# A recurrence's twenty head sums, set into a stream of projections in pairs

## The chip, the cores and the metric

The kernel runs on one core of one Trainium2 chip. The metric is the device time of one execution in microseconds (us), where lower is better. A core has engines with instruction streams of their own: TensorE (PE, with its weight loads as PEld), VectorE (DVE), ScalarE (ACT), GpSimd (POOL) and SyncE (SP, which mostly issues DMAs). [...] An instruction that waits holds up everything behind it on its engine.

## The reference

One layer of a hybrid diffusion backbone is applied to 128 context tokens and to 512 latent tokens. The kernel lays them out as 640 tokens, five tiles of 128. Cut to what matters here:

```python
proj = h @ lw['w_in']
(a_x, a_b, a_c, b_q, b_ff, b_fb, b_i, b_g, c_q, c_k, c_v, d_u, d_v) = jnp.split(proj, IN_SPLITS, axis=-1)
y_a = a_b * dwconv3(a_c * a_x, lw['conv_a_w'], lw['conv_a_b'])
y_b, s_f, s_b = hgrn2_bidir(b_q, b_ff, b_fb, b_i, b_g, lb_f, lb_b, ...)    # the recurrence
...                                                                        # y_c attention, y_d gMLP
merged = g_a * (y_a @ w_br_a) + g_b * (y_b @ w_br_b) + g_c * (y_c @ w_br_c) + g_d * (y_d @ w_br_d)
x = x + g1 * (merged @ lw['w_o'])
x = x + g2 * conv_ffn(rmsnorm(x, ...) * (1.0 + sc2) + sh2, ...)
```

`hgrn2_bidir` is a gated linear recurrence in both directions over four heads of 64. With decays f = exp(log_f), its output is, for each token t, a sum over earlier tokens s of (q_t · k_s · product of the decays between them) times v_s, plus the same from later tokens, plus what the carried state of 64 x 64 gives. The final context states are an output too.

## The kernel before, in words

All matrix products of the layer are made from split f32 operands: a weight tile is split into a high and a low part (`w`, split by ACT at L323 or L336 and by DVE at L324 or L337), activations into `XH` and `XL`, and three matmuls make one product. The input projections `h @ w_in` come first. They run section by section (`in_tile`, through `gemm_half`, whose matmuls are recorded at L375, 320 tokens wide) and for the sections `i` and `dv` token by token (`tok_tile`, L947, 256 wide).

The mixers are written as Python generators that are advanced while the projections are issued: after each group of three projection matmuls, the code calls `tick(us)` with the time that these three are planned to take (0.41 in `gemm_half`, 0.33 in `tok_tile`). `tick` moves a planned clock on and advances each generator whose next step is due. A generator's `yield x` says that its next step is due x planned us (times a slack factor, 1.3 for the recurrence) after its present one. So a generator's yields decide behind which projection matmul its next instructions stand. The instruction order that results is then fixed, apart from what the tile framework's own scheduler exchanges among ready instructions. Small products take a PSUM buffer from a pool of four (`pm`, tile names `m_…`), the projections from a pool of two (`g_…`).

Several generators share this stream. `hgrn` is the recurrence and starts when its `q` section is done. `ada_cols` makes modulation columns: weight tiles are loaded by SP and multiplied and summed on DVE at L285, 1.2 us each. `gmlp` is the chunked gMLP (L694, L704, L709), and `attn` the attention, which is started behind the last input section and is the next large user of PE (L762 onward).

The recurrence works by doubling: level l joins blocks of 2^l tokens into blocks twice as long. Its steps, in the order of the code:

- the products of keys and queries, on DVE (L469 to L491);
- `along(ksum)`, and from its result the diagonal of the block matrix on DVE (L497);
- level 0: `along(near)`, and a masked copy by DVE into the same block matrix (L520);
- levels 1 to 6: products of keys and queries on PE (L539), a masked copy of each on DVE (L544) or a copy on ACT (L548), then the updates of the decayed keys, queries and decays on DVE (L558, L562) and copies of keys (L506 on DVE, L507 on ACT);
- the state, for four pairs of tiles: `kt_load` transposes two key tiles on PE (L578), ACT copies each (L581), `upd` multiplies them with the values on PE (L587), and DVE adds each result to the decayed state (L598; the context's copies at L595);
- the outputs of five token tiles on PE (L632, L634, L639), copied and squared on ACT (L643, L644), normalised with DVE and POOL (L648, L318, L623), then transposed (L661) and gated (L665), and stored (L668).

`along(x)` makes ten head sums: each is one matmul with a 128 x 128 tile of `x` as weights and the two columns of `heads` as moving operand (L479, 128x2). All ten fall into one PSUM buffer, which DVE reads once, after the tenth. It is called twice, so there are twenty sums. At `yield 0.5`, a step is due 0.65 planned us after the one before.

Of the kernel before, what the change touches and what calls it, by code (L numbers as in the profile page):

```python
# [70 lines left out]
def tile_step(ctx: ExitStack, tc: tile.TileContext, a: dict, outs: list, dbg=None):  # L71
# [21 lines left out]
    def pe(us):  # L93
        now[0] += us
# [38 lines left out]
    def pm():  # L133
        return psm.tile([P, 512], F32, tag="m", name=nm("m"))
# [74 lines left out]
    for x in LORD.split():  # L209
        if x[0] == "w":  # L210
            i, h = int(x[1]), int(x[2])
# [248 lines left out]
    def hgrn():  # L460
# [13 lines left out]
        def along(x):  # L474

            m = pm()
            mv = m[:, 0:20].rearrange("p (r i) -> p i r", r=2)
            for i in range(10):
                mm(mv[:, i, :], x[:, i * P:(i + 1) * P], heads, start=True, stop=True)  # L479
                pe(0.22)  # L480
                yield 0.5
            return m


# [5 lines left out]
        for j in range(2):  # L490
            vec.tensor_tensor(n2[:, j], k2(j)[:, j], q2(1 - j)[:, 1 - j], ALU.mult)  # L491
        dm = yield from along(ksum)

        near_at = hd[:, 1280:1920].rearrange("p (r i t) -> p r i t", r=2, i=10)
# [17 lines left out]
        for l in range(7):  # L512
# [5 lines left out]
            if l == 0:  # L518
                m = yield from along(near)
                vec.copy_predicated(nat, lmask[:, 0, :].unsqueeze(1).to_broadcast([P, 20, 32]), bc(m))  # L520
# [1943 lines left out]
```

## Time and profile before

| what | value |
|---|---|
| median of 3 runs | 1006.01 us (1005.86 to 1006.21) |
| the profiled execution's own time | 1005.19 us |
| its span | 1003.4 us |
| granted TensorE clock in each stage from 78 us on | 1.00 |
| PE busy | 992.1 us, 99% of the span, 7509 matmuls |
| DVE busy | 823.6 us, 82% |
| ACT busy | 559.4 us, 56% |
| POOL busy | 165.8 us, 17% |
| the twenty head sums on PE | first call 78.9 to 84.1 us, second call 92.0 to 102.0 us |

The span lies between the first and the last recorded work; 1.8 us of the execution's time lie outside it. A timeline row reads: start, time, engine, line, operation, output<-input, shapes, and how many such instructions stand together. A bracket behind it gives the idle time of the engine ahead of it and what ended that. One f32 head sum shows as two matmuls in the trace.

### The profile page before, as it was taken

What the parts mean: (1) busy time and instruction counts of PE and PEld (TensorE: products, weight loads), DVE (VectorE), ACT (ScalarE), POOL (GpSimd) and SP (SyncE); (2) the same over time, 40 slices, a digit from 0 to 9 for tenths busy, and PEclk for the clock granted to TensorE, in tenths of its full rate; (3) what the DMA queues carried; (4) which work ended last, traced back from release to release, by engine and by line L of the source; (5) the groups of instructions that cost most, each with busy time, mean ns of one, the idle gap of its engine ahead of it and who ended that gap; (6) DMA issues with size and microseconds to landing.
All of it is one profiled execution on the core that took longest, in us unless ns stands there. A gap on an engine that the chain in (4) does not pass through costs nothing.

```text
span 1003.4 us, 18971 instructions
## 1 busy us (share of the span) xinstructions
PE 992.1 (99%) x7509; PEld 941.0 (94%) x7509; DVE 823.6 (82%) x1383; ACT 559.4 (56%) x983; POOL 165.8 (17%) x223
## 2 busy tenths in 40 slices
PE   8999999999999999999999999999999999999997
PEld 6899999999999999999998899999999999888886
DVE  6678899867766767777768878999999998999796
ACT  6642343444544544445545376777777777756672
POOL 1000020323120221341010021222222222100004
PEclk9999999999999999999999999999999999999998
DMA  9875343497485498898259675766666666975842
GB/s 354 333 251 160 116 148 123 127 253 226 106 282 201 159 252 180 271 291 182 93 173 347 277 290 170 229 154 174 174 161 171 177 169 194 364 259 205 298 134 105
DMA packets 69865, 208.93 MB, mean 208 GB/s; under 512 B 9616, under 2 KB 24752, under 8 KB 67088
## 3 DMA queue, kind: packets, MB, share of 16 engines
q1 hardware_dynamic: 43392, 148.60, 41.7%
q0 software_dynamic: 26384, 59.12, 25.3%
q8 instruction: 59, 0.97, 0.4%
q14 instruction: 30, 0.25, 0.1%
HBM read 165.99 MB, written 48.51 MB: 214 GB/s over the span
## 4 chain that ended last, share of the span: by engine, by line
PE 93%; DVE 3%; DMA 2%; issue 1%; POOL 1%; ACT 1%; SPq 0%; POOLq 0%; ACTq 0%; DVEq 0%
PE g L1523 21%; PE m L1152 17%; PE g L375 15%; PE m L1995 9%; PE m L1523 5%; PE g L1165 5%; PE g L1995 4%; PE m L1295 3%; PE g L947 2%; PE g L1295 2%; PE m L151 2%; PE g L151 1%; PE m L539 1%; PE m L1518 1%; DMA A<-in_w_ada_dram 1%
## 5 line engine op out<-in xcount | busy, mean ns | idle before, releaser
L375 PE MATMUL g<-XH,w 128*128 128x320 f32 x704 | 171.2, 317 | 0.1
L375 PEld LDWEIGHTS g<-XH,w 128*128 128x128 f32 x704 | 120.6, 188 | 2.7 <-issue 1.0
L375 PE MATMUL g<-XL,w 128*128 128x320 f32 x352 | 108.7, 309 | 0.0
L375 PEld LDWEIGHTS g<-XL,w 128*128 128x128 f32 x352 | 66.3, 188 | 0.0
L1995 PE MATMUL m<-w,XH 128*128 128x512 f32 x246 | 58.5, 390 | 0.0
L1995 PEld LDWEIGHTS m<-w,XH 128*128 128x128 f32 x246 | 46.1, 188 | 9.6
L1152 PE MATMUL m<-XH,w 128*128 128x320 f32 x224 | 52.5, 309 | 0.0
L151 POOL DMA_DIRECT2D wsum<-in_w_dn_dram x36 | 36.5, 1164 | 53.2 <-issue 42.3
L151 DVE SCALAR_TENSOR_TENSOR X<-MG,p2t,X 128x641 f32<-128x641 f32 x44 | 38.9, 884 | 1.0 <-ACT X L151 0.2
L151 ACT ACTIVATE w<-raw 128x1024 fp32r<-128x1024 f32 (+3 forms) x46 | 38.2, 851 | 2.6 <-DMA raw<-in_w_in_dram 1.5
L151 DVE SCALAR_TENSOR_TENSOR X<-X,p2t,X 128x641 f32<-128x641 f32 x44 | 38.9, 883 | 0.9
L1523 PE MATMUL g<-XL,w 128*128 128x320 f32 x240 | 38.7, 310 | 0.0
L1152 PEld LDWEIGHTS m<-XH,w 128*128 128x128 f32 x224 | 38.3, 188 | 0.0
L1523 PE MATMUL g<-XL,C 128*128 128x320 f32 x240 | 38.3, 309 | 0.0
L1523 PEld LDWEIGHTS g<-XL,w 128*128 128x128 f32 x240 | 36.0, 188 | 0.6 <-ACT MG L151 0.3
L1523 PEld LDWEIGHTS g<-XL,C 128*128 128x128 f32 x240 | 36.0, 188 | 0.0
L151 ACT ACTIVATE ga<-m,cst 128x320 f32<-128x320 f32 x27 | 14.2, 528 | 36.6 <-PE m L1152 36.6
L1152 PE MATMUL m<-XL,w 128*128 128x320 f32 x112 | 34.6, 309 | 0.0
L151 DVE TENSOR_TENSOR w<-raw,w 128x1024 fp32r<-128x1024 f32 (+2 forms) x36 | 30.6, 871 | 1.3 <-ACT w L151 1.2
L151 DVE TENSOR_TENSOR gb<-g,gb 128x640 f32<-128x640 f32 x12 | 9.9, 825 | 26.3 <-PE g L1165 25.4
L1894 DVE TENSOR_TENSOR w<-raw,w 128x1024 fp32r<-128x1024 f32 (+1 forms) x26 | 29.0, 1114 | 2.6 <-ACT w L1890 2.6
L336 ACT ACTIVATE w<-raw 128x1024 fp32r<-128x1024 f32 (+1 forms) x22 | 24.3, 1104 | 12.2 <-PE m L947 8.2
(591 smaller groups left out, 2918.4 us busy)
## 6 DMA issues: line engine op xcount, KB each, us to landing
wsum<-in_w_dn_dram POOLq DMA_DIRECT2D x30, 512.0 KB, 11.8
raw<-in_w_up_dram SPq DMA_DIRECT2D x30, 512.0 KB, 5.1
raw<-in_w_gp_dram SPq DMA_DIRECT2D x21, 640.0 KB, 6.7
raw<-in_w_in_dram SPq DMA_DIRECT2D x19, 512.0 KB, 4.2
H<-in_w_adt_dram SPq DMA_DIRECT2D x19, 512.0 KB, 3.8
raw<-wsum SPq DMA_DIRECT2D x12, 512.0 KB, 5.4
actx<-X POOLq DMA_DIRECT2D x22, 256.0 KB, 4.9
wsum<-wsum POOLq DMA_DIRECT2D x10, 512.0 KB, 11.0
```

The costliest lines, as they stand in the source:

```text
L151: r = f(*args, **kw)
L336: high = lambda: act(w[:, 0], raw, AF.Copy)
L375: mm(o, w[:, h, k0 + k, :], r(k)[:, s], start=(k == 0 and i == 0), stop=(k == kt - 1 and i == 2))
L539: mm(m[W * g:W * g + W, (i - s0) * W:(i - s0 + 1) * W], lhs, rhs, start=True, stop=True, tile_position=(64 * par, W * g))
L947: mm(o, x(kx)[:, ts], w[:, h, k, :], start=(kx == 0 and i == 0), stop=(kx == 7 and i == 2))
L1152: mm(o, w[:, k, :], x[:, k, :], start=(first and k == 0 and j == 0), stop=(k == 3 and j == 2), skip_group_check=True)
L1165: mm(pb[:, c, 0:HC], w[:, h + k, :], y[:, x, k, s], start=(k == 0 and j == 0), stop=(k == 1 and j == 2))
L1295: mm(m, mh[k // 2][:, hx, k % 2, t * P:(t + 1) * P], wo[q][:, hw, k % 2, :], start=(k == 0 and i == 0), stop=(k == 7 and i == 2))
L1518: mm(o, w[:, k, :], x[:, k, :], start=(first and not part and k == 0 and j == 0), stop=(part == 1 and k == 3), skip_group_check=True)
L1523: z = mm(o, w[:, k, :], x[:, k, :], start=(first and k == 0 and j == 0), stop=(k == 3 and j == 2), skip_group_check=True)
L1894: vec.tensor_tensor(w[:, 1, 0:n], raw, w[:, 0, 0:n].bitcast(F32), ALU.subtract)
L1995: mm(ps, s[t // 4][:, hx, k, o:o + P], w[:, hw, k, c0:c1], start=first, stop=i == 2 and bi == len(batch) - 1 and k == len(ks) - 1, skip_gr ...
```

## The change

The pause behind each sum is replaced by one behind each second sum. `[1.2] * (i % 2)` is empty for even i and one element for odd i, so that two sums are issued in one step, and the next step is due 1.2 x 1.3 = 1.56 planned us later.

```diff
             for i in range(10):
                 mm(mv[:, i, :], x[:, i * P:(i + 1) * P], heads, start=True, stop=True)
                 pe(0.22)
-                yield 0.5
+                yield from [1.2] * (i % 2)
             return m
```

In the second call the projections around the sums are those of L375. In PE's order before, each sum (L479) stands alone between projection matmuls:

```order
L375 MATMUL g_1190<-XH_255,w_1012 128x320
L479 MATMUL m_1230<-heads,E_1020 128x2
L375 MATMUL g_1190<-XH_255,w_1012 128x320
L375 MATMUL g_1190<-XL_15_256,w_1012 128x320
L375 MATMUL g_1190<-XH_255,w_1012 128x320 x2
L375 MATMUL g_1190<-XL_16_257,w_1012 128x320
L375 MATMUL g_1190<-XH_255,w_1012 128x320
L479 MATMUL m_1230<-heads,E_1020 128x2
L375 MATMUL g_1190<-XH_255,w_1012 128x320
```

The same place in PE's order of the changed kernel (`m_1230` is the one PSUM buffer of the ten sums, `E_1020` holds `near`):

```order
L479 MATMUL m_1230<-heads,E_1020 128x2 x2
L375 MATMUL g_1190<-XH_255,w_1012 128x320
L375 MATMUL g_1190<-XL_15_256,w_1012 128x320
L375 MATMUL g_1190<-XH_255,w_1012 128x320 x2
L375 MATMUL g_1190<-XL_16_257,w_1012 128x320
L375 MATMUL g_1190<-XH_255,w_1012 128x320 x2
L375 MATMUL g_1190<-XL_16_257,w_1012 128x320
L375 MATMUL g_1190<-XH_255,w_1012 128x320
L479 MATMUL m_1230<-heads,E_1020 128x2 x2
```

Ten single sums with six projection matmuls between them have become five pairs with nine. The last sum of the second call stands 18 projection matmuls earlier than before. In the first call, amid `tok_tile`, the sums stand almost where they stood. What follows the second call moves with it: the products of levels 1 to 5 (L539) stand about 15 projection matmuls earlier. On DVE this moves the masked copies of level 1 (L544) against the rest of its order; this is the difference there, with - for before and + for the changed kernel:

```order
 L558 TENSOR_TENSOR B_797<-B_797,A_796 128x320x2 x2
 L506 COPY E_1020<-B_797 128x160x4
-L544 COPY_PREDICATED D_943<-lmask,m_1400 128x320
-L337 TENSOR_TENSOR w_1494<-raw_1258,w_1494 128x1024
-L544 COPY_PREDICATED D_943<-lmask,m_1445 128x320
+L544 COPY_PREDICATED D_943<-lmask,m_1382 128x320
+L544 COPY_PREDICATED D_943<-lmask,m_1427 128x320
 L558 TENSOR_TENSOR C_1037<-C_1037,A_796 128x320x2 x2
 L562 TENSOR_TENSOR A_796<-A_796 128x640
-L285 SCALAR_TENSOR_TENSOR junk_1531,ar_1532<-H_1265,S_82_887 128x1024
 L558 TENSOR_TENSOR B_797<-B_797,A_796 128x160x4
```

The subtraction that makes a low weight part (L337) now stands behind both masked copies and the updates. The third place is the first pair of the state update on PE. Before, the four transposes (L578) stand together, and twelve projection matmuls separate them from the products (L587):

```order
L578 MATMUL m_2331<-cst,B_797 128x128 x2
L578 MATMUL m_2335<-cst,B_797 128x128 x2
L375 MATMUL g_2347<-XH_255,w_1992 128x320
L375 MATMUL g_2347<-XL_15_256,w_1992 128x320
L375 MATMUL g_2347<-XH_255,w_1992 128x320 x2
L375 MATMUL g_2347<-XL_15_256,w_1992 128x320
L375 MATMUL g_2347<-XH_255,w_1992 128x320 x2
L375 MATMUL g_2347<-XL_15_256,w_1992 128x320
L375 MATMUL g_2347<-XH_255,w_1992 128x320 x2
L375 MATMUL g_2347<-XL_15_256,w_1992 128x320
L375 MATMUL g_2347<-XH_255,w_1992 128x320
L587 MATMUL m_2365<-E_1020,D_943 128x128 x2
```

In the changed kernel:

```order
L578 MATMUL m_2303<-cst,B_797 128x128 x2
L375 MATMUL g_2219<-XH_255,w_1874 128x320 x2
L375 MATMUL g_2219<-XL_15_256,w_1874 128x320
L578 MATMUL m_2307<-cst,B_797 128x128 x2
L587 MATMUL m_2324<-E_1020,D_943 128x128 x2
L375 MATMUL g_2219<-XH_255,w_1874 128x320
L587 MATMUL m_2331<-E_1020,D_943 128x128 x2
L375 MATMUL g_2219<-XH_255,w_1874 128x320
L375 MATMUL g_2219<-XL_16_257,w_1874 128x320
L375 MATMUL g_2219<-XH_255,w_1874 128x320
L578 MATMUL m_2349<-cst,B_797 128x128 x2
```

The two transposes of each tile now stand apart, and the first product directly behind the second tile's transposes. Over all, the steps of the state update and the outputs stand 2 to 4 us' worth of projection matmuls earlier. The attention (L762) stands behind the same projection matmul as before. No instruction of the computation is added or removed.

## The prediction

> **What bounds the kernel now.** I read the page first: the busy shares, and the shares of the chain that ended last.
>
> ```profile
> PE 992.1 (99%) x7509; PEld 941.0 (94%) x7509; DVE 823.6 (82%) x1383; ACT 559.4 (56%) x983; POOL 165.8 (17%) x223
> PE 93%; DVE 3%; DMA 2%; issue 1%; POOL 1%; ACT 1%; SPq 0%; POOLq 0%; ACTq 0%; DVEq 0%
> ```
>
> TensorE has matmuls for 99% of the span and carries 93% of the last chain. The waits of PE over the whole run come next (waiting, releaser, total us, times, longest):
>
> ```profile
> PE g L151 <- DVE F L151: 1.6, 1, 1.6
> PE m L151 <- DMA A<-in_w_ada_dram: 1.5, 2, 0.8
> PE m L151 <- DVE X L151: 1.1, 4, 0.3
> PE m L661 <- DVE MG L665: 0.2, 1, 0.2
> ```
>
> That is 4.4 us in all. Only the last, 0.2 us, lies where the recurrence runs. By stages (length, then busy time of PE, its loads, DVE, ACT and POOL, then granted clock, DMA share, GB/s):
>
> ```profile
> 78.00:104.00 26.00, 26.00 (x201) 26.00 (x200) 21.96 (x36) 6.68 (x11) 0.00 (x0) 1.00 0.49 155
> 104.00:160.00 56.00, 55.90 (x1205) 51.25 (x1205) 52.36 (x96) 24.76 (x51) 5.17 (x6) 1.00 0.40 125
> 160.00:190.00 30.00, 30.00 (x235) 29.87 (x235) 27.50 (x70) 9.08 (x26) 2.02 (x2) 1.00 0.41 126
> 190.00:208.00 18.00, 17.84 (x124) 17.41 (x123) 13.49 (x31) 9.04 (x18) 8.39 (x8) 1.00 0.72 195
> ```
>
> From 78 to 208 us, in which everything lies that the change moves, PE idles 0.10 + 0.16 = 0.26 us, and the granted clock is 1.00 throughout. DVE is nearly full there too: 52.36 of 56 and 27.50 of 30. So the time of this stretch is what its matmuls cost back to back. A new order can change it in three ways only: by what the matmuls cost in that order, by taking away 0.26 us of idling, or by making PE wait. The attention behind it stands behind the same projection matmul as before, so a recurrence that ends earlier does not bring the attention forward.
>
> **The sums themselves.** A projection matmul's price comes from two runs of them in the chain (start, us, what, how many), 21.12/144 = 0.147 us and 5.75/48 = 0.120 us:
>
> ```profile
> 49.63 21.12 PE g L375 x144
> 103.64 5.75 PE g L947 x48
> ```
>
> A sum alone, and a pair that the scheduler had already put together in the first call, from PE's timeline:
>
> ```profile
> 96.44 0.28 PE L479 MATMUL m<-heads,E 128*128 128x2 f32 x2
> 96.58 0.39 PE L375 MATMUL g<-XH,w 128*128 128x320 f32 x1
> 96.81 0.31 PE L375 MATMUL g<-XL,w 128*128 128x320 f32 x1
> ...
> 80.11 0.50 PE L479 MATMUL m<-heads,D 128*128 128x2 f32 x4
> 80.48 0.37 PE L947 MATMUL g<-w,XH 128*128 128x256 f32 x1
> 80.68 0.28 PE L947 MATMUL g<-w,XL 128*128 128x256 f32 x1
> ```
>
> I count from start to start. From the single sum to the second projection matmul behind it are 96.81 - 96.44 = 0.37 us, of which 0.147 is the first one's regular price: the sum costs 0.22. Of that, 0.14 is its own, and 0.08 is the return, since the first projection matmul behind it takes 0.23 and not 0.147. The pair: 80.68 - 80.11 = 0.57, less 0.12, makes 0.45. So two sums together cost as much as two apart. Ten singles were 2.2 us and five pairs are 2.25: **+0.05**. The lower bound is that each pair saves a whole return, 5 x 0.08: -0.4. The upper one is +0.05, since nothing in these rows makes a pair dearer than measured. I take +0.05, because its row shows the very thing that is added.
>
> [...]
>
> **The steps behind the sums.** These stand earlier among the projections, 15 matmuls at levels 1 to 5 (15 x 0.147 = 2.2 us) and up to 24 in the state update (3.5 us). The same matmuls are still issued; what was behind them is now ahead. Two things cost. The scheduler splits groups: between the first sum and the attention, PE returns to the projections, not counting the sums, 38 times before and 43 times now. Five returns at 0.08 are **+0.4**. The bounds are 0, if the displaced steps only trade one return for another, and +0.5 by the dearest return in the rows below (164.38 - 164.14 = 0.24, so 0.09 over the regular price, rounded up to 0.1 each).
>
> The second thing: the first product of the state (L587) stands three projection matmuls behind the transposes it depends on, through ACT's copy (L581), where twelve stood before. From the timelines of PE and ACT:
>
> ```profile
> 163.79 0.60 PE L578 MATMUL m<-cst,B 128*128 128x128 f32 x4
> 164.14 0.40 PE L375 MATMUL g<-XH,w 128*128 128x320 f32 x1
> 164.38 0.30 PE L375 MATMUL g<-XL,w 128*128 128x320 f32 x1
> ...
> 165.99 0.72 PE L587 MATMUL m<-E,D 128*128 128x128 f32 x5
> ...
> 171.71 0.68 PE L578 MATMUL m<-cst,B 128*128 128x128 f32 x4
> ```
>
> ```profile
> 172.18 0.69 ACT L581 ACTIVATE D<-m 128x256 f32<-128x256 f32 x2 [3.29 <-PE m L578]
> ```
>
> ACT begins 172.18 - 171.71 = 0.47 after the transposes began, and two copies take 0.69, so the first is there about 0.47 + 0.38 = 0.85 us after them (0.38 being an estimate, half of 0.69 and a little overlap). PE takes 0.35 for four transposes, so 0.18 for two, then 0.08 + 3 x 0.147, then 0.18 for the second tile: it arrives after about 0.88. The copy and its signal come about there: between 0 and 0.4 of waiting. I take **+0.2**. What goes: the 0.26 us of idling, by at most all of it; I take **-0.2**.
>
> **What hides the rest.** PE can only stay full if DVE follows, since the small PSUM buffers come free through DVE. Three of DVE's waits of over a microsecond between 78 and 190 us, and then some of its timeline:
>
> ```profile
> DVE D L544 <- PE m L539: 2.5, 1, 2.5
> DVE w L337 <- ACT w L336: 1.2, 1, 1.2
> DVE D L520 <- PE m L479: 1.2, 1, 1.2
> ```
>
> ```profile
> 164.57 1.22 DVE L285 SCALAR_TENSOR_TENSOR junk<-X,S 128x1024 bf16<-128x1024 f32 x1
> ...
> 169.52 2.37 DVE L598 SCALAR_TENSOR_TENSOR D<-D,tot,m 64x64 f32<-64x64 f32 x8
> ...
> 178.50 2.07 DVE L598 SCALAR_TENSOR_TENSOR D<-D,tot,m 64x64 f32<-64x64 f32 x7
> ```
>
> The first state product starts at 165.99, and DVE takes it up at 169.52: DVE is 3.5 us behind PE there, and only the four buffers keep PE going. If PE comes up to 3.5 us earlier and DVE does not, PE waits. But DVE was late because it had waited itself, 2.5 us for the first product of level 1 and 1.2 us for a weight's high part. The first shrinks by the 2.2 us that PE comes earlier; the second goes, as that subtraction now stands behind both masked copies. So DVE comes 2.2 + 1.2 = 3.4 us earlier. The first buffer that is reused belongs to the third pair of transposes (171.71 before, 24 matmuls earlier now: 168.2). It comes free with the first half of the first L598, 169.52 + 1.19 = 170.7 before, 167.3 now. That leaves 0.9 us, and **0** is what I enter. ACT (9.08 us of 30) and the queues (DMA share 0.40 to 0.41 up to 190 us) have room. SP and POOL keep their instructions; their orders differ only from about 100 to 270 us, where loads of modulation weights and the store of y_b, now some 4 us earlier, fall into 0.41 and 0.72 of the DMA engines.
>
> The sum: +0.05 + 0.4 + 0.2 - 0.2 + 0 = +0.45 us. On the profiled execution, 1005.19 us, of which the span is 1003.4, that makes 1005.64. That execution lies 0.82 below the median of the runs, 1006.01, so against medians I expect 1006.5 us. A measurement here tells about 0.2%, 2 us, from no change. The forecast's own range is 1005.2 (sums at -0.4, returns and copy at 0, all idling gone, so 1006.01 - 0.66, and 0.15 for the spread of the runs shown) to 1007.0 (+0.05 + 0.5 + 0.4 = +0.95).
>
> **The rivals.**
>
> *PE waits for DVE in the state update (slower).* Place: the third pair of transposes. If DVE gains nothing, because its 52 us of work in the levels fill the time and the products of L285 (1.22 us each) slip ahead of the recurrence's own steps, as three of them would to use up 3.4 us, PE waits from 168.2 to 170.7, 2.5 us. The later waits are not added to this: the output's first matmul on the last state needs 178.50 + 2.07 = 180.57, and PE is then no earlier than that. So 1006.46 + 2.5 = 1009.0 us. It begins once DVE gains under 2.5 us there, and passes 2 us in all once DVE gains under about 1. For it: DVE's busy share, and that the order of its products and of the weights' subtractions is changed over 80 us. Against: the removed waits are DVE's own, and no L285 is added before the first L598.
>
> *The lead is kept to the end (faster).* The 2.2 us by which level 1 comes earlier would shorten the run if something behind the recurrence waited for it: 1006.0 - 2.2 = 1003.8. Against: PE idles 0.16 us from 190 to 208, so nothing waits there to be released.
>
> [...]
>
> *The change does less than it says.* In the first call the scheduler had joined sums already (80.11, four matmuls), and there nothing moves. If the splits on PE cost nothing either, 1006.0.
>
> **How the numbers follow.** My forecast has a chance of 0.60, the free pair 0.05 and the idle change 0.05; all three lie within 0.2%: 0.70. PE waiting for DVE has 0.22, as the reserve is only 0.9 us, less than one L285, and rests on an order of some 200 instructions on DVE that no trace here shows. The kept lead has 0.08, including any gain whose way I don't see. The range goes from 1005.2, the forecast's lower end, to 1009.2, which takes in most of the slower case; it leaves out the faster one and the part of the slower where waits add up, under 0.2 together.
>
> **What would show it.** In the changed profile, PE should have about 130 us busy from 78 to 208 with under 0.5 us idle. L479 pairs should take 0.45 us each, ending about 2.6 us earlier (18 x 0.147). The first L544 should start near 109.1 and the first L598 near 166, with no wait of PE on DVE at L578 or L587 above 0.3 us. A wait of PE at L578, L587 or L632 for L598 of a microsecond or more makes me wrong on the slow side; the attention's first L762 more than 1 us earlier makes me wrong on the fast side.

## The result and the profile after

The changed kernel takes 1011.69 us (median of 4 runs, 1009.33 to 1012.66) against 1005.93 us before (4 runs). The ratio is 1.0059, with a 95% interval of 1.0047 to 1.0071: slower by 5.8 us (0.6%), where I had forecast 1006.5 and a range up to 1009.2. The profiled execution is the one of 1012.66 us; its span is 1010.9 us, 7.5 longer than before. Busy shares on the page first:

```profile
PE 995.7 (98%) x7509; PEld 943.7 (93%) x7509; DVE 825.0 (82%) x1383; ACT 560.0 (55%) x983; POOL 166.8 (17%) x223
```

The same 7509 matmuls, but PE is busy for 3.6 us more, so some of them ran slower; the other half of the 7.5 us must be idling. PE's waits of the changed kernel between 78 and 210 us say where:

```profile
PE m L661 <- DVE MG L665: 2.1, 1, 2.1
PE m L539 <- issue: 1.7, 1, 1.7
```

Before, there was one row of 0.2 us. The stages carry the rest of it; the column to read is the granted clock, the third from the right:

```profile
78.00:104.00 26.00, 26.00 (x201) 26.00 (x200) 22.57 (x37) 6.68 (x11) 0.00 (x0) 1.00 0.47 152
104.00:160.00 56.00, 54.20 (x1175) 49.86 (x1173) 51.17 (x87) 24.67 (x51) 5.09 (x6) 0.97 0.35 115
160.00:190.00 30.00, 30.00 (x236) 28.70 (x236) 28.49 (x74) 9.40 (x25) 1.85 (x1) 1.00 0.38 122
190.00:208.00 18.00, 15.86 (x104) 15.48 (x103) 13.69 (x35) 6.53 (x13) 8.59 (x8) 0.94 0.72 206
```

The stage with the pairs is as full as before, at full clock. The losses lie in the two stages behind it: 1.8 and 2.1 us of idling, and in both a clock below 1. PE's timeline at the first stop, inside a group of 80 small products of level 1, and the clock behind it:

```profile
109.56 0.74 PE L539 MATMUL m<-C,D 64*32 64x32 f32 x62
112.00 0.37 PE L539 MATMUL m<-C,D 64*32 64x32 f32 x18 [1.70 <-issue]
```

```profile
113.00:114.00 1.00, 1.00 (x9) 1.00 (x8) 1.00 (x2) 0.00 (x0) 0.00 (x0) 0.77 0.06 16
114.00:116.00 2.00, 2.00 (x12) 1.94 (x11) 1.97 (x3) 0.36 (x1) 0.00 (x0) 0.50 0.00 0
116.00:117.00 1.00, 1.00 (x6) 1.00 (x6) 0.77 (x2) 0.85 (x2) 0.00 (x0) 0.53 0.00 0
```

The releaser "issue" means that the profile shows nothing that holds PE in these 1.70 us: no semaphore, no buffer. After that the clock column shows 0.50; the trace's clock records put this window from 113.53 to 116.94 us, 3.41 us. The projection matmuls in it start 0.213 us apart (three from 114.29 to 114.93 us), where they start 0.120 us apart at full clock:

```profile
114.29 0.41 PE L947 MATMUL m<-w,XL 128*128 128x256 f32 x1
114.50 0.63 PE L947 MATMUL m<-w,XH 128*128 128x256 f32 x2
114.93 0.41 PE L947 MATMUL m<-w,XL 128*128 128x256 f32 x1
```

So PE does 3.41 x 0.120 / 0.213 = 1.9 us' worth of work in the window, and the window costs 1.5 us. The second stop is at the transposes, again with a window of 3.41 us at half clock behind it (205.7 to 209.1 us):

```profile
204.46 0.33 PE L661 MATMUL m<-cst,MG 128*128 128x128 f32 x1 [2.14 <-DVE MG L665]
```

```profile
205.00:206.00 1.00, 1.00 (x9) 0.99 (x8) 0.98 (x5) 0.20 (x1) 0.00 (x0) 0.84 1.24 367
206.00:208.00 2.00, 2.00 (x10) 1.92 (x9) 0.67 (x3) 2.00 (x5) 1.41 (x2) 0.50 0.95 389
208.00:209.00 1.00, 1.00 (x5) 1.00 (x5) 0.35 (x1) 0.88 (x2) 0.17 (x1) 0.50 0.46 184
```

1.7 + 2.1 of stops and 2 x 1.5 of half clock are 6.8 of the 7.5 us. The other 0.7 is about what e5 below shows the new order to cost where nothing stops. Some landmarks, as PE's timelines give the first matmul of a line (us):

```
                        before   after   after again (e11)   both edits (e5)
L539, level 1           110.40  108.18        108.17             108.16
L661, transposes        200.50  200.65        198.96             202.00
L762, attention         208.69  216.24        213.04             209.48
L1152                   308.97  316.53        313.35             309.77
```

Level 1 comes 2.2 us earlier, as worked out. That the figure fits is partly chance: level 1 stands 18 projection matmuls earlier and not 15, and those just ahead of it are of the 0.120 us kind (18 x 0.120 = 2.2); levels 3 to 5 stand 15 earlier. At the attention everything lost is there, and from L762 to L1152 both take 100.28 or 100.29 us.

Why does DVE come late to the transposes? Its timeline before, and then the changed kernel's:

```profile
196.48 0.42 DVE L623 TENSOR_TENSOR MG<-MG,hss 128x256 f32<-128x256 f32 x1 [0.93 <-POOL hss L318]
196.82 1.49 DVE L676 TENSOR_TENSOR E<-X,E 128x1280 fp32r<-128x1280 f32 x1
198.23 1.22 DVE L285 SCALAR_TENSOR_TENSOR junk<-H,S 128x1024 bf16<-128x1024 f32 x1
...
201.08 1.13 DVE L665 SCALAR_TENSOR_TENSOR MG<-m,cst,MG 128x128 f32<-128x128 f32 x3
```

```profile
198.13 0.43 DVE L623 TENSOR_TENSOR MG<-MG,hss 128x256 f32<-128x256 f32 x1 [0.89 <-POOL hss L318]
...
201.32 1.22 DVE L285 SCALAR_TENSOR_TENSOR H<-H,S 128x1024 f32<-128x1024 f32 x1
...
202.79 1.22 DVE L285 SCALAR_TENSOR_TENSOR junk<-A,S 128x1024 bf16<-128x1024 f32 x1
203.93 0.08 DVE L285 DVE_READ_ACCUMULATOR junk<-A,S 128x1 f32 x1
204.05 2.27 DVE L665 SCALAR_TENSOR_TENSOR MG<-m,cst,MG 128x128 f32<-128x128 f32 x8
```

From the last L598 to the first L665, DVE has eight products of L285 in the changed kernel and six before. Two more (2.4 us) have slipped in there, the last one directly ahead of L665. The first of PE's transposes stands 27 projection matmuls earlier, the one that waits 22 earlier than the one that waited before. It waits for the PSUM buffer that L665 has to read.

### The profile page after: what moved, and what is told of

The parts are those of the page before. It is cut to its first block, busy times and chain, and to the rows that moved or that the text cites. A ratio compares the mean times of both kernels' runs of the same rounds, so it can differ in the third digit from the quotient of the medians.

```text
span 1010.9 us, 18975 instructions
## 1 busy us (share of the span) xinstructions
PE 995.7 (98%) x7509; PEld 943.7 (93%) x7509; DVE 825.0 (82%) x1383; ACT 560.0 (55%) x983; POOL 166.8 (17%) x223
## 4 chain that ended last, share of the span: by engine, by line
PE 95%; DMA 2%; DVE 1%; issue 1%; ACT 1%; POOL 0%; SPq 0%; POOLq 0%; ACTq 0%; DVEq 0%
PE g L1523 21%; PE m L1152 17%; PE g L375 16%; PE m L1995 9%; PE m L1523 5%; PE g L1165 5%; PE g L1995 4%; PE m L1295 3%; PE g L947 2%; PE g L1295 2%; PE m L151 2%; PE g L151 1%; PE m L539 1%; PE m L1518 1%; DMA A<-in_w_ada_dram 1%
## 5 line engine op out<-in xcount | busy, mean ns | idle before, releaser
L375 PE MATMUL g<-XH,w 128*128 128x320 f32 x704 | 170.3, 318 | 0.1
L375 PEld LDWEIGHTS g<-XH,w 128*128 128x128 f32 x704 | 121.2, 189 | 2.7 <-issue 1.0
L375 PE MATMUL g<-XL,w 128*128 128x320 f32 x352 | 109.9, 312 | 0.0
L375 PEld LDWEIGHTS g<-XL,w 128*128 128x128 f32 x352 | 66.8, 190 | 0.2
L1152 PE MATMUL m<-XH,w 128*128 128x320 f32 x224 | 52.5, 309 | 0.0
L1523 PE MATMUL g<-XL,w 128*128 128x320 f32 x240 | 38.6, 310 | 0.0
L1523 PE MATMUL g<-XL,C 128*128 128x320 f32 x240 | 38.3, 309 | 0.0
L1152 PEld LDWEIGHTS m<-XH,w 128*128 128x128 f32 x224 | 38.3, 188 | 0.0
L1523 PEld LDWEIGHTS g<-XL,w 128*128 128x128 f32 x240 | 35.9, 188 | 0.7 <-ACT MG L151 0.3
L1523 PEld LDWEIGHTS g<-XL,C 128*128 128x128 f32 x240 | 36.0, 188 | 0.0
L1152 PE MATMUL m<-XL,w 128*128 128x320 f32 x112 | 34.6, 309 | 0.0
```

The lines of the kernel that those rows point to most:

```text
L375: mm(o, w[:, h, k0 + k, :], r(k)[:, s], start=(k == 0 and i == 0), stop=(k == kt - 1 and i == 2))
L1152: mm(o, w[:, k, :], x[:, k, :], start=(first and k == 0 and j == 0), stop=(k == 3 and j == 2), skip_group_check=True)
L1523: z = mm(o, w[:, k, :], x[:, k, :], start=(first and k == 0 and j == 0), stop=(k == 3 and j == 2), skip_group_check=True)
```

## The experiments

Theory A: the loss is the two stops and the half clock behind them. Theory B: the pairs, or the split groups on PE, cost it. Theory C: the stop at L539 hangs on its place in the work (a load, a buffer), and not on the instruction fetch.

**e1: single sums, as early as the pairs.** First, pairing is taken apart from earliness.

```diff
-                yield from [1.2] * (i % 2)
+                yield 0.5 if x is ksum else (0.25, 0.25, 0.5, 0.25, 0.25, 0.5, 0.25, 0.25, 0.5, 0.95)[i]
```

> Ten single sums, as in the kernel before, but issued at the pace that brings the tenth to where the pairs bring it; everything behind the sums stands where the changed kernel has it. Theory A (the loss comes from two stops of PE behind the sums, one in the products of level 1 and one at the transposes L661, and from the half clock behind each): as slow as the changed kernel, 1009 to 1012.7 us, with a stop of about 2 us at L661 and, in most executions, one of about 1.7 us at L539. Theory B (the pairs themselves cost it): as fast as before, 1006 us.

1012.29 us, ratio 1.0065 (1.0052 to 1.0078). PE's waits from 78 to 215 us:

```profile
PE m L661 <- DVE MG L665: 2.2, 1, 2.2
PE m L539 <- issue: 1.3, 1, 1.3
```

Without a single pair in the second call, the loss is all there, at the same two places. Theory B falls for the pairs.

**e9: pairs, with all else in place.** The converse: pairs in the second call, their last where the last single sum was.

```diff
         def along(x):
-
+            yield from [0.5] * (x is not ksum)
...
-                yield from [1.2] * (i % 2)
+                yield from [0.5] if x is ksum else [1.45 if i < 9 else 0.8] * (i % 2)
```

> The kernel before with the ten sums of the second call as five pairs, spaced so that the tenth sum and all that follows it stand where they stand in the kernel before. Theory A (the pairs cost nothing, what moved behind them did): 1005 to 1005.8 us, no stop of PE between 78 and 208 us. Theory B (the pairs cost it): 1006.5 us or more.

1005.16 us against 1005.21, ratio 0.9999 (0.9990 to 1.0007). The stretch as a whole:

```profile
78.00:208.00 130.00, 129.74 (x1758) 124.53 (x1758) 115.28 (x230) 49.58 (x103) 15.54 (x16) 1.00 0.47 141
```

So pairs as such cost and save nothing.

**e4 and e7: the transposes moved.** In e4 they go back in the changed kernel; in e7 they come forward in the kernel before. Both are one number.

```diff
 # e4, in the changed kernel
-HY = 5
+HY = 8
 # e7, in the kernel before
-HY = 5
+HY = 2
```

> The changed kernel with HY = 8 in place of 5: the transposes L661 stand 30 projection matmuls later, 3 behind their place in the kernel before; the level products stay early. Theory A: the stop at L661 goes with the half clock behind it, some 3.8 us less than the changed kernel in the same execution conditions, and what is left is the stop at L539: 1006.5 to 1010 us. Theory B: no change against the changed kernel, 1009 to 1012.7 us.

> The kernel before, single sums, with HY = 2 in place of 5: only the transposes L661 stand earlier, by 27 projection matmuls (4.0 us), as in the changed kernel, and one L285 slips ahead of the first L665 on DVE. Theory A: a stop at L661 of 3 to 4.5 us, more than in the changed kernel since DVE has not come earlier here, often with half clock behind it: 1008.5 to 1011.5 us. Theory B: 1005 to 1006 us.

e4: 1008.80 us, ratio 1.0033 (1.0023 to 1.0044). The stop at L661 is gone, that at L539 is there (1.6 us); the time is 3.5 us below e1's, which was measured in the same series and has both stops. e7: 1012.39 us, ratio 1.0068 (1.0054 to 1.0082), beyond what I expected (1011.5 at most, with a stop of 3 to 4.5 us), by one stop and its clock:

```profile
PE m L661 <- DVE MG L665: 5.2, 1, 5.2
```

```profile
201.00:204.00 3.00, 0.76 (x3) 0.76 (x4) 2.62 (x8) 0.00 (x0) 0.00 (x0) 0.51 1.01 310
204.00:207.00 3.00, 3.00 (x14) 2.85 (x14) 1.33 (x5) 0.00 (x0) 1.42 (x2) 0.50 0.85 320
```

That shows the cause of the second stop from both sides: transposes 4 us earlier, with a DVE that does not follow. The length of e7's stop is the sum of both. Its first L665 starts at 202.84 us against 201.08 before; everything in that profile stands 0.67 us later from the second call of sums on, so DVE is 1.1 us late, with seven L285 in place of six ahead of L665. The delay of 1.09, the 27 projection matmuls at 0.147 (3.97) and the wait of before (0.16) are 5.2 us.

**e2 and e3: the code moved.** Both leave the order alone and change only how many instructions stand ahead of it, by PE's warm-up matmuls at the start.

```diff
 # e2, in the changed kernel
-WARM = 100
+WARM = 118
 # e3, in the kernel before
-WARM = 100
+WARM = 82
```

> The changed kernel with 118 in place of 100 warm-up matmuls at the very start, which PE spends waiting for data anyway: 36 instructions more ahead of everything, so that the level-1 products stand to PE's 16 KB instruction fetches as they do in the kernel before. Theory A, with the stop at L539 being a late instruction fetch: that stop goes, with the half clock behind it, some 3.5 us; PE then comes to L661 earlier, and the stop there grows by up to what DVE has not gained, so 1007 to 1010 us. Theory C (the stop at L539 comes from something that hangs on the place in the projections, such as a load or a buffer): it stays, 1009 to 1012.7 us.

> The kernel before with 82 in place of 100 warm-up matmuls: 36 instructions fewer, so that its level-1 products stand to the instruction fetches as they do in the changed kernel; the order of all else is that of before. Theory A: a stop of 1 to 2 us at L539 with half clock behind it appears, 1008.5 to 1010 us. Theory C: unchanged, 1006 us.

e2: 1013.52 us, ratio 1.0071 (1.0055 to 1.0088). The stop at L539 is gone, that at L661 is unchanged:

```profile
PE m L661 <- DVE MG L665: 2.2, 1, 2.2
PE m L539 <- DVE C L558: 0.3, 1, 0.3
```

The time missed its expectation all the same: it is no lower than e1's 1012.29 us in the same series, which has both stops. So e2 shows what the stop at L539 hangs on, and not that the kernel gains without it. Its profiled execution (1010.48 us) has a window at half clock at 81.7 us, in the first call of sums, with no stop ahead of it, and loses another 0.9 us behind 840 us, where PE waits twice for 0.2 us at L1523. Its slower runs are not explained by that profile. e3: 1006.07 us, ratio 1.0006 (0.9997 to 1.0014). A stop appears at L539 where before had none, but of 0.3 us and without half clock, so the expected 1008.5 was missed. In theory A's favour is the place, against my size for it the length.

**e6 and e10: pairs that come later, and their code moved.**

```diff
 # e6 and e10
-                yield from [1.2] * (i % 2)
+                yield from [1.45] * (i % 2)
 # e10 also
-... tu1a warm24 xo0b ...
+... tu1a warm34 xo0b ...
-WARM = 100
+WARM = 118
```

> The pairs as in the changed kernel, but with 1.45 in place of 1.2, one group of projection matmuls more between them: the tenth sum of the second call stands 6 projection matmuls behind its place before, the level-1 products 15 behind, the first L661 9 behind. Theory A: no stop at either place, 1005 to 1006.5 us. Theory B: the pairs cost as in the changed kernel, 1009 us or more.

> The pairs with 1.45, which had a stop of 1.8 us in the products of level 2, with 28 more warm-up matmuls at the start (118 in place of 100, 34 in place of 24): 56 instructions more ahead of everything, so that level 2 begins 29 instructions behind the place where the fetch that ran late begins, and not 27 ahead of it. Theory A (late instruction fetch): no stop in level 1 or 2, 1005 to 1007 us. Theory C (a load, a buffer or DVE behind the stop): the stop stays at the same matmul of level 2, 1007 to 1009.6 us.

e6: 1008.51 us, ratio 1.0031 (1.0020 to 1.0043); e10: 1009.20 us, ratio 1.0035 (1.0023 to 1.0047). Both missed their times, and both by a stop with the releaser "issue" at a new place, the first of level 2, the second of level 5:

```profile
121.54 0.84 PE L539 MATMUL m<-C,E 64*32 64x32 f32 x75
124.19 0.32 PE L539 MATMUL m<-C,E 64*32 64x32 f32 x5 [1.80 <-issue]
```

```profile
147.57 0.84 PE L539 MATMUL m<-C,B 64*32 64x32 f32 x74
149.86 0.26 PE L539 MATMUL m<-C,B 64*32 64x32 f32 x6 [1.46 <-issue]
```

The trace also records the transfers of instructions (`q8 instruction: 59, 0.97, 0.4%` in the DMA view of both kernels: packets, MB, share of 16 engines). They are 59 of 16,384 bytes in the kernel before and in the changed one, where PE has some 15,100 recorded instructions: one transfer for 256 on average. The record names no engine for them; from this quotient I take them for PE's, and call them fetches. I counted PE's recorded instructions (matmuls, weight loads and its few semaphore instructions) up to three events:

```
kernel       dense group(s) begin   fetch begins at      PE stops at
before       1987                   1952 (108.07 us)     no stop
e2, e5, e8   1987                   1950 to 1952         no stop at level 1
e9           1987                   1974 (109.21 us)     no stop
after        1951                   2123 (109.58 us)     2240
after again  1951                   2063 (108.65 us)     2240
e1, e4       1951                   2113, 2114           2240
e3           1951                   1951 (110.11 us)     2240 (0.3 us)
e6           2436, level 2          2658 (121.76 us)     2752
e10          3718, level 5          3883 (147.22 us)     4032
```

Every stop with the releaser "issue", in seven profiles, falls on 2240 plus a multiple of 256: 2752 is 2 x 256 further, 4032 is 7 x 256. As 256 is also the number of instructions to one transfer, I take PE to have stood there for want of instructions; that is inferred from the counts, and no record shows it directly. It speaks against theory C that e10 took the stop away from level 2 by 56 instructions at the start, some 100 us earlier. Why it happens here I read from a projection matmul's 0.147 us and a level product's 0.011 us (80 in 0.89 us): by these, 300 instructions, half of them weight loads, are an estimated 20 us of projections but 2 us of two dense groups. A fetch takes from 0.9 us (e1) to 1.8 us (before); in the seven profiles with a stop it lands 1.3 to 1.6 us before PE goes on (110.55 and 112.00 after), so that 2.4 to 2.8 us pass from its start. In the changed kernel PE goes from 1952, where the fetch begins in the kernel before, to 2240 in 1.9 us (108.18 to 110.11); in the kernel before it takes 4.0 us (108.16 to 112.15). Set against the 2.4 us and more from a fetch's start to where PE goes on, those 1.9 us are too short, by a little even where the fetch is prompt, and by more where it begins late. In e3 it began when PE got there, and the stop was 0.3 us; in e11 it began 0.5 us after, in the changed kernel 1.4 us after, and the stops were 1.1 and 1.7 us. That the fetch begins late needs no load in its way: in e6 the DMA share was 0.00 from 118 to 121 us. Nor does it need a dense group: in e9 the same fetch began 1.3 us after PE got to 1952 (107.95 us), amid projections, where 22 instructions went by and nothing stopped. Why it begins later in some executions stays open.

**e5 and e8: both edits.** HY = 8 (e5) or 6.5 (e8), and 118 warm-up matmuls, in the changed kernel.

> The changed kernel, pairs and early level products kept, with both edits: HY = 8 (transposes L661 back behind DVE) and 118 warm-up matmuls (instruction fetches moved). Theory A: neither stop, attention's first matmul (L762) within 1.5 us of before's 208.7, or 3.2 us where one window at half clock still falls somewhere; 1005 to 1008 us. Theory B (pairs, or the splits on PE, cost it): still 1009 us or more with PE busy all the way.

> As the kernel with both edits, but HY = 6.5: the transposes L661 stand 15 projection matmuls (2.2 us) later than in the changed kernel and 12 before their place in the kernel before, and the extra L285 is no longer ahead of L665. Theory A: the stop of 2.3 us at L661 shrinks to under 0.5 us: 1005 to 1008 us. If the stop hangs on something other than DVE's place: 1008 to 1010 us.

e5: 1007.13 us (1005.93 to 1010.09), ratio 1.0022 (1.0013 to 1.0031). Its profiled execution of 1005.93 us has one wait of 0.3 us from 78 to 215, the clock at 1.00, and the attention 0.8 us later than before. So 0.8 us is what the new order costs in that execution, where nothing stops for longer. The median lies 2.0 us above the kernel before, so 1.2 us of it this profile does not show. Against e4 (1.0033), which keeps the stop at L539, the gain is about 1 us by the ratios, and the two intervals overlap: what that stop costs is read from the profiles, and not from the medians. e8: 1009.96 us (4 runs), ratio 1.0050 (1.0034 to 1.0065), a miss in time. In its profile the transposes no longer wait, as expected of 2.2 us more room; that execution's 1008.39 us lies 3.2 above the median before. 1.3 us of it are there at L762 (209.98 us), 2.1 at L1152 (311.08 us), and the other 1.1 us is added behind 840 us, where PE waits for 0.4 and 0.2 us at L1523 and the kernel before does not wait. Why it waits there is open. The slower runs of both kernels are not explained by these profiles.

**e11: the changed kernel again.**

> The changed kernel once more, for a second profile. Theory A: the stops at L539 and L661 come back at the same instructions and with nearly the same lengths (1.7 and 2.1 us), since they hang on the order; whether one, both or none is followed by a window at half clock differs from execution to execution: 1009.2 us without, 1.7 more for each window.

1009.52 us, one run. The same two stops, at the same instructions (2240 and, for L661, 4883 in both profiles), and no window at half clock:

```profile
PE m L661 <- DVE MG L665: 2.2, 1, 2.2
PE m L539 <- issue: 1.1, 1, 1.1
PE m L539 <- DVE C L558: 0.3, 1, 0.3
```

```profile
78.00:208.00 130.00, 126.35 (x1728) 120.30 (x1728) 116.19 (x231) 49.17 (x99) 16.36 (x16) 1.00 0.45 139
```

So the stops belong to the order: they are there in both profiles. The half clock comes or not. L762 stands 3.2 us earlier here than in the first profile; the shorter first stop, less the new 0.3 us wait, is 0.3 of that, and the two windows are the other 2.9, 1.5 us each. The four runs of the changed kernel fit that step: 1009.33, 1010.93, 1012.45 and 1012.66 us, with mean granted clocks of 0.998, 0.996, 0.995 and 0.995. e9's runs lie within 1.0 us.

## Why the prediction was wrong

- **The sums, +0.05.** Right. The pairs took 0.44 us each (99.61 - 99.02 = 0.59, less 0.147):

```profile
99.02 0.50 PE L479 MATMUL m<-heads,E 128*128 128x2 f32 x4
99.38 0.39 PE L375 MATMUL g<-XH,w 128*128 128x320 f32 x1
99.61 0.31 PE L375 MATMUL g<-XL,w 128*128 128x320 f32 x1
```

e9 shows the sum over all pairs to be nothing that can be measured. The free pair, which has a chance of 0.05 in the forecast, is out: no run shows a second sum that costs nearly nothing, two took 0.44 us where one took 0.22.

- **Returns +0.4, ACT's copy +0.2, idling -0.2.** Near in size together: +0.8 in e5 where I had 0.4, with 0.3 of it a wait of level 6 for L558 that I hadn't seen. Which of the three terms gave the rest is not shown, except that there was no wait for ACT's copy.

- **DVE comes 3.4 us earlier.** Right as far as I followed it. The first L544 stood at 109.12 us, as forecast (109.1). In e5, where no stop is in the way, the first L598 is at 166.06, forecast near 166:

```profile
166.06 0.27 DVE L598 SCALAR_TENSOR_TENSOR D<-D,tot,m 64x64 f32<-64x64 f32 x1
```

No wait at L578 or L632 appeared, so the rival of a waiting PE was priced at the wrong place.

- **"What hides the rest."** This is the step that failed. I followed DVE's lead to the state update and entered 0 for all behind it. But I had myself written that the steps up to the outputs stand 2 to 4 us earlier, and L661 is the one place in this stretch where PE had waited for DVE before (0.2 us, the row is quoted). There the reserve was nothing. DVE's lead did not last: 3.4 us at the first L598, 2.0 us at the last (178.25 us in e5 against 180.28), and the two L285 more in between take 2.4 us. e2 shows it, where the stop at L539 is gone; its early window had put everything 1.4 us later by the second call of sums (first sum at 93.39 us, against 91.98 in the changed kernel's first profile). With that taken off, DVE reaches the first L665 at 201.04 us, against 201.08 before, no earlier at all. PE reaches the transpose that waits at 199.26 us, against 201.33 before, 2.1 us earlier. With the 0.2 us of before, that makes the 2.2 us of e2's wait. The term entered at 0 measured 2.1 to 2.2 us.

- **"A new order can change it in three ways only."** There is a fourth, and I had no term for it: the order also set where dense groups of small matmuls stand to the instruction transfers, and with that came stops of 0.3 to 1.8 us in seven profiles. Nothing in the profile of before shows a stop for it, but its records of instruction transfers were there to be read.

- **The clock.** I took 1.00 as given. In some executions a stop of 1.3 to 2.1 us came with a window of 3.41 us at half clock: up to 1.5 us on top, nearly as much again as the stop. The shortest stops with a window behind them were 1.3 us in e1 and 1.46 us in e10. Each window lasted 3.41 us, or twice that in e7, and the changed kernel's two profiles differ in whether one comes; what decides that is not shown.

The rival of a kept lead is out: L762 came earlier in none of the kernels whose level products stand earlier.

## What to carry to other kernels

On PE, busy for 99%, moving work earlier gained nothing by itself (1007.13 us in e5, which has neither stop, against 1005.16). Each consumer that is moved has to be checked against its producer's own order to the very end of what moves, first of all where a small wait already stands: 0.2 us at L661 became 2.1 to 2.2, and 5.2 in e7. Dense runs of tiny matmuls had a price here that no dependency shows, 0.3 to 1.8 us: look up the instruction transfers in the trace, and how such runs stand to them. In some executions here, a stop of one or two microseconds on PE cost up to 1.5 us more through the clock.

## What the runs showed of the hardware that I had not expected

- PE stood for 0.3 to 1.8 us at L539 with nothing in the profile that held it, always at one of three counts of instructions (2240, 2752, 4032), which lie multiples of 256 apart. 36 instructions more ahead of everything removed such a stop from a place 100 us later (e2), and 56 more moved one from level 2 to level 5 (e6, e10).
- A stop of PE came with a window at half clock in some executions and not in others: with one in profiles with stops of 1.3, 1.5, 1.7, 1.8 and 2.1 us, without one after stops of 1.1, 1.6 and 2.2 us; the changed kernel's two profiles differ in this. In a window of the changed kernel a projection matmul of L947 took 0.213 us in place of 0.120. Each window lasted 3.41 us, or 6.83 us, twice that, from 201.1 us on in e7, whose stop of 5.2 us ended at 203.2. One window came with no stop ahead of it, at 81.7 us in e2, amid the first call of sums. Its cause is open.
